# Gathering the experts' tokens by indirect DMA instead of one-hot products, with pairs overlapped by one and a larger weight ring

## The chip, the core and the metric

The kernel runs on one core of one Trainium2 chip. The metric is the device time of one execution in microseconds (us). The core has five engines with an instruction queue each: TensorE (PE, its weight loads PEld), VectorE (DVE), ScalarE (ACT), GpSimd (POOL) and SyncE (SP, which here mainly issues DMAs). ScalarE and POOL can issue DMAs too. Instructions of one queue start in order; between engines, semaphores decide.

## The reference

Two blocks in a row work on 512 tokens of width 1024. The first block (two layers of attention and MLP) and the mixer of the second aren't touched. The change lies in the second block's mixture of experts, which is the last part:

```python
    g_idx = jnp.argmax(g_logits, axis=-1)
...
    top_v, top_i = lax.top_k(e_sel, TOP_K)
    gate = jax.nn.softmax(top_v, axis=-1) * p_g[:, None]
...
    def run(args):
        tok_b, e = args
        xb = v_pad[tok_b]
        hu = xb @ w_e_in[e]
        a, u = jnp.split(hu, 2, axis=-1)
        return (jax.nn.silu(a) * u) @ w_e_out[e]
...
    ys = ys * rows_w[:, None].astype(ys.dtype)
    out = jnp.zeros((T + 1, D), ys.dtype).at[rows_tok].add(ys)
```

A token's group is one of 4, and its two experts are the best of the group's 8. For each of the 32 experts e, w_e_in[e] is 1024 x 1024 and w_e_out[e] 512 x 1024, all in float32. The results, weighted by the gates, are added to the tokens, and a last RMS norm follows.

## The kernel before

The 32 experts are worked in 16 pairs, q = 0 to 15. In a pair each expert has 64 places for tokens; one expert of pair 8 (`SPARE` = 16) is chosen for having most tokens and has a further job of 128 places, the overflow job. More overflow is handled by a loop at the end that runs as often as needed.

`project` comes first. For each of four tiles t of 128 tokens it makes the output product of the mixer (`product`, lines 1410 to 1412) and adds it to `acc` (L1416); `norm` squares (L1421) and makes the root; `flip` transposes `acc` on TensorE (L1434); `logits` multiplies by the router; `select` finds group and experts on VectorE (L1549 to L1590, among them the small TENSOR_SCALAR L1577), `route` numbers the places (L1598 to L1602), and `rows` writes the normalised tokens as two parts, vrh and vrl, for products in two passes: ScalarE makes vrh (L1450), and vrl comes from VectorE for t = 0, 1 (L1452) and from POOL for t = 2, 3 (L1456, after ScalarE's copy L1455). The tiles follow each other without a gap on TensorE: `flip` of one tile stands inside the `product` of the next.

For two pairs at a time, `prepare` makes one-hot tables P of tokens to places on VectorE (`places`), and `gather` multiplies vrh and vrl by them (`collect`, L1735, 64 products of 128 x 256 a time), which gives the transposed tokens X (`store`, L1744 and L1746, times the norm's gain). `expert` then makes the hidden products pa and pu (L1761, 64 a pair, each of two experts on half of the array's columns), the gated activation H, transposes H (L1781), makes the output products py (L1789, 32), scales them by the gate into yh and yl (L1794, L1795), and scatters them into `acc` by the table PT (L1802 to L1804). These steps are generators, and the loop over q in `moe` interleaves them: the scatter of one pair runs beside the hidden products of the next, the gather of pairs q + 2 and q + 3 between the two halves of q and q + 1.

Weights come from `moe_weights`: tiles of 512 KB (128 x 1024 float32), 16 of e_in and 8 of e_out a pair, 384 in all, into a ring of 3 tiles wraw and 26 tiles ew, in the order in which they are used. All are issued by SP (L1523, the last ones as halves, L1527), in order; a load waits until the tile in its place has been used. Part of the ring lies where the mixer's tiles `wo` and `mix` lay, so those loads wait for the last products that read these. Every DMA of the kernel, whichever engine issues it, has one of eight counters, DMAHW0 to DMAHW7, dealt in turn in the order of the program, and waits until the DMA that had this counter before has landed.

## Time and profile before

| what | value |
|---|---|
| median of three runs | 2528.14 us (2528.12 to 2528.62) |
| the profiled execution | 2530.76 us |
| its span in the profile | 2529.0 us |
| mean granted clock of TensorE | 0.989 of full speed |
| TensorE busy | 2458.7 us, 97% of the span |
| VectorE, ScalarE, POOL busy | 59%, 46%, 4% of the span |
| moved by DMA | 361.67 MB, mean 143 GB/s |

A time is counted from the start of the span. `project` starts near 1927, the first expert's hidden products near 2000, and the end of the span is 2529. The profile's two strips of 40 slices (63 us each) show how DMA and TensorE share this last part: TensorE stands at 9 tenths nearly everywhere, and the DMA strip rises from 1 to 3 tenths to 5 to 9 only in the last ten slices, that is from about 1900 on.

The tables by stretches further down have a line for each stretch: its bounds, its length, then for each engine its busy time and, in brackets with an x, its instructions, in the order PE, PEld, DVE, ACT, POOL; then the mean granted clock of TensorE as a share, the DMA engines' busy share and what they moved in GB/s. Where a line of code is chosen, the busy times are those of that line's instructions alone (PE and PEld for a product). A row of a timeline gives the start, the length, engine, line, operation, out<-in by the program's names, shapes and the count; brackets at its end give the idle time before it and who ended it. For SP's queue the length of a row with a count spans all of its issues.

### The profile page before, as it was taken

The page shows a single profiled execution, that of the slowest core. Times are in us where ns is not written, and L with a number is a line of the kernel's source. Part 1 is how long each engine was busy: PE and PEld are TensorE (multiplying, and loading weights), DVE is VectorE, ACT ScalarE, POOL GpSimd, SP SyncE. Part 2 cuts the span into 40 slices and gives each one's busy share as a digit, 9 for nine tenths or more (in the row PEclk, how much of TensorE's full clock was granted, in tenths as well). Part 3 has the DMA queues.
Part 4 walks back from the last instruction along what each step waited for, and adds up shares of the span by engine and source line. Part 5 has one row for each costly group of instructions (what it writes and reads, how often), then busy time and mean ns, then how long its engine had stood idle before and what let it go on. Part 6 is the DMA issues. An engine that isn't in the chain of part 4 may idle for free. (4 is left out here: it accounts for less than half of the span.)

```text
span 2529.0 us, 38832 instructions
## 1 busy us (share of the span) xinstructions
PE 2458.7 (97%) x15048; PEld 1981.4 (78%) x15048; DVE 1480.9 (59%) x2797; ACT 1150.9 (46%) x2181; POOL 98.3 (4%) x83
## 2 busy tenths in 40 slices
PE   8999999999989899999999999999999999999997
PEld 8999999999977777788887988998888744444442
DVE  6666654344589986533445658888653654434435
ACT  6777643233367776422334656655553311112112
POOL 0000000000133220000000000000000000000000
PEclk9999999999999999999999999999999999999998
DMA  3111232222321113232333212121336599978995
GB/s 119 51 51 39 72 93 91 92 92 92 119 69 44 50 35 107 95 100 92 93 99 116 69 59 67 59 67 55 97 120 238 209 394 406 409 297 336 409 409 211
DMA packets 110139, 361.67 MB, mean 143 GB/s; under 512 B 13440, under 2 KB 17792, under 8 KB 109952
## 3 DMA queue, kind: packets, MB, share of 16 engines
q1 hardware_dynamic: 109376, 357.05, 39.7%
q8 instruction: 120, 1.97, 0.3%
q10 hardware_dynamic: 576, 2.10, 0.2%
q14 instruction: 67, 0.55, 0.1%
HBM read 352.75 MB, written 6.36 MB: 142 GB/s over the span
## 5 line engine op out<-in xcount | busy, mean ns | idle before, releaser
L172 PE MATMUL dn<-hg_hi,whi 128*128 128x264 f32 (+1 forms) x2096 | 680.3, 325 | 9.2 <-ACT hg_hi L293 6.7
L173 PE MATMUL dn<-hg_lo,whi 128*128 128x264 f32 (+1 forms) x2096 | 666.1, 318 | 2.1 <-DVE hg_lo L294 2.0
L174 PE MATMUL dn<-hg_hi,wlo 128*128 128x264 f32 (+1 forms) x2096 | 666.3, 318 | 0.0
L144 ACT ACTIVATE whi<-wraw 128x1024 fp32r<-128x1024 f32 (+1 forms) x285 | 284.8, 999 | 606.6 <-PE dn L173 529.6
L172 PEld LDWEIGHTS dn<-hg_hi,whi 128*128 128x128 f32 x2096 | 399.9, 191 | 37.6 <-ACT hg_hi L293 6.7
L173 PEld LDWEIGHTS dn<-hg_lo,whi 128*128 128x128 f32 x2096 | 399.8, 191 | 31.7 <-DVE hg_lo L294 4.3
L174 PEld LDWEIGHTS dn<-hg_hi,wlo 128*128 128x128 f32 x2096 | 399.9, 191 | 24.8
L145 DVE TENSOR_TENSOR wlo<-wraw,whi 128x1024 fp32r<-128x1024 f32 (+1 forms) x285 | 332.3, 1166 | 91.8 <-ACT whi L144 90.4
L172 PE MATMUL dn<-rhi,whi 128*128 128x264 f32 (+1 forms) x768 | 247.0, 322 | 2.2 <-DVE h L202 1.7
L174 PE MATMUL dn<-rhi,wlo 128*128 128x264 f32 (+1 forms) x768 | 246.8, 321 | 0.0
L173 PE MATMUL dn<-rlo,whi 128*128 128x264 f32 (+1 forms) x768 | 246.7, 321 | 0.0
L202 DVE TENSOR_TENSOR h<-h,dn 128x264 f32<-128x264 f32 (+1 forms) x120 | 61.8, 515 | 199.6 <-PE dn L174 199.3
L172 PEld LDWEIGHTS dn<-rhi,whi 128*128 128x128 f32 x768 | 144.4, 188 | 14.8 <-DVE h L202 2.9
L173 PEld LDWEIGHTS dn<-rlo,whi 128*128 128x128 f32 x768 | 144.5, 188 | 11.4
L174 PEld LDWEIGHTS dn<-rhi,wlo 128*128 128x128 f32 x768 | 144.5, 188 | 11.1
L1761 PE MATMUL pa<-ew,X 128*64 128x512 f32 (+1 forms) x470 | 130.7, 595 | 1.9 <-DVE H L1766 1.9
L1761 PE MATMUL pu<-ew,X 128*64 128x512 f32 (+1 forms) x470 | 130.6, 594 | 0.0
L367 DVE SCALAR_TENSOR_TENSOR relu<-dn,rstd 128x264 f32<-128x264 f32 (+1 forms) x93 | 48.2, 519 | 130.3 <-PE dn L174 130.3
L1019 DVE SCALAR_TENSOR_TENSOR H<-pa,PTq 128x512 f32<-128x512 f32 x17 | 11.7, 691 | 187.1 <-ACT PTq L1018 173.6
L1789 PE MATMUL py<-ew,HT 128*64 128x512 f32 (+1 forms) x472 | 112.4, 595 | 0.7 <-ACT HT L1783 0.7
L1804 DVE TENSOR_TENSOR acc<-acc,g 128x512 f32<-128x512 f32 x136 | 86.1, 680 | 35.1 <-PE g L1803 35.1
L1016 ACT ACTIVATE PTq<-pa 128x512 f32<-128x512 f32 x17 | 10.2, 597 | 197.5 <-PE pa L1761 197.5
(545 smaller groups left out, 4373.0 us busy)
## 6 DMA issues: line engine op xcount, KB each, us to landing
ew<-e_in SPq DMA_DIRECT2D x228, 512.0 KB, 10.1
ew<-e_out SPq DMA_DIRECT2D x109, 512.0 KB, 10.1
wraw<-mlp_in SPq DMA_DIRECT2D x64, 512.0 KB, 3.5
wraw<-mlp_out SPq DMA_DIRECT2D x64, 512.0 KB, 3.4
wraw<-w SPq DMA_DIRECT2D x60, 512.0 KB, 3.5
wraw<-e_in SPq DMA_DIRECT2D x28, 512.0 KB, 10.1
wraw<-a_qkv SPq DMA_DIRECT2D x24, 512.0 KB, 3.5
wraw<-kv SPq DMA_DIRECT2D x16, 512.0 KB, 3.5
```

The source lines that it names most:

```text
L144: nc.scalar.activation(hi, raw, AF.Copy)
L145: nc.vector.tensor_sub(lo, raw, hi)
L172: nc.tensor.matmul(ps, whi[:, k, :], hi[:, a:b], start=(k == 0), stop=False)
L173: nc.tensor.matmul(ps, whi[:, k, :], lo[:, a:b], start=False, stop=False)
L174: nc.tensor.matmul(ps, wlo[:, k, :], hi[:, a:b], start=False, stop=(k == len(act) - 1))
L202: self.nc.vector.tensor_add(self.h[:, t, a:b], self.h[:, t, a:b], ps)
L367: nc.vector.scalar_tensor_tensor(x, ps, 0.0, self.rstd[:, a:b], op0=ALU.max, op1=ALU.mult)
L1016: nc.scalar.activation(t, x, AF.Abs)
L1019: nc.vector.scalar_tensor_tensor(out, x, 0.0, t, op0=ALU.min, op1=ALU.subtract)
L1761: nc.tensor.matmul(ps[r], X[i][:, k, :], win[i][k][:, c:c + 512], start=(k == 0), stop=(k == KT - 1), skip_group_check=True)
L1789: nc.tensor.matmul(ys[c][r], HT[:, k, r], wout[i][k][:, c * 512:c * 512 + 512], start=(k == 0), stop=(k == 3), skip_group_check=True)
L1804: nc.vector.tensor_add(self.acc[:, t, cs], self.acc[:, t, cs], po)
```

## The change

`rows` now makes a float32 copy x of every tile of tokens on ScalarE (L1458), multiplies it on POOL by -0.5 times the norm's gain (`grow`, L1463), and writes it to a DRAM buffer `vbuf` by a DMA of ScalarE's queue (L1464). `prepare` now belongs to one job: it makes PT as before, then the token number of each place (`at`) by one more pass over PT with an accumulator, clears a tile `rows` on POOL (L1757) and fills it by an indirect DMA of POOL's queue from `vbuf` (L1758), in which places without a token have an index out of bounds and are skipped. `tokens` transposes `rows` by eight TensorE transposes (L1773) and copies into X. The one-hot products stay only for pairs 0 and 1. The generators are gone: the loop takes jobs 0 to 8, the overflow, 9 to 15, and for job n issues hidden(n), then turned(n-1) (the transposes of H), tokens(n+1), scatter(n-2), prepare(n+2), results(n-1). The loads are reordered accordingly, with a pair's e_in ahead of the e_out of the pair before. The ring has 31 instead of 26 ew tiles, 34 places in all; vrh and vrl move to a pool that ends with `project`.

```diff
-        self.vr = [rp.tile([128, 4, D], F32R, name="vr" + nm) for nm in "hl"]
+        self.vr = [rt.tile([128, 4, D], F32R, name="vr" + nm) for nm in "hl"]
+        gr = rt.tile([128, D], F32, name="grow")
+        src = self.w["g_ffn"]
+        nc.sync.dma_start(gr, bass.AP(tensor=src.tensor, offset=src.offset, ap=[[0, 128], [1, D]]))
+        nc.gpsimd.tensor_scalar(gr, gr, -0.5, None, op0=ALU.mult)
...
         def rows(t):
             hi, lo = self.vr[0][:, t, :], self.vr[1][:, t, :]
             nc.scalar.activation(hi, self.acc[:, t, :], AF.Copy, scale=rs[t])
+            x = rt.tile([128, D], F32, name="vrow", bufs=2)
+            nc.scalar.activation(x, self.acc[:, t, :], AF.Copy, scale=rs[t])
             if t < self.RP:
                 nc.vector.scalar_tensor_tensor(lo, self.acc[:, t, :], rs[t], hi, op0=ALU.mult, op1=ALU.subtract)
             else:
-                x = rt.tile([128, D], F32, name="vrow")
-                nc.scalar.activation(x, self.acc[:, t, :], AF.Copy, scale=rs[t])
                 nc.gpsimd.tensor_sub(lo, x, hi)
+            nc.gpsimd.tensor_mul(x, x, gr)
+            nc.scalar.dma_start(self.vbuf[t * 128:(t + 1) * 128, :], x)
...
-        for q, i in [(q, i) for q in range(14) for i in range(2)] + [(14, 0), (15, 0), (14, 1), (15, 1)]:
-            yield from load(q, *sides[i], 2 if (q, i) == (15, 1) else 1)
+        jobs = self.jobs()
+        for q, p in zip(jobs + [None], [None] + jobs):
+            if q is not None:
+                yield from load(q, self.w["e_in"], KT, 1)
+            if p is not None:
+                yield from load(p, self.w["e_out"], 4, 2 if p == 15 else 1)
...
+    def prepare(self, slot):
...
+        nc.vector.tensor_scalar(q, self.kb[:, 0, :], slot, None, op0=ALU.is_equal)
+        nc.vector.scalar_tensor_tensor(PT, self.kb[:, 1, :], slot, q, op0=ALU.is_equal, op1=ALU.add)
+        nc.vector.scalar_tensor_tensor(q, PT.bitcast(F32), 1.0, self.tok, op0=ALU.mult, op1=ALU.mult,
+                                       accum_out=gs[:, 3:4])
+
+        at = wk.tile([128, 1], U32, name="at", bufs=2)
+        nc.vector.tensor_scalar(at, gs[:, 3:4], float(S), None, op0=ALU.add)
+        rows = wk.tile([128, D], F32, name="rows", bufs=2)
+        nc.gpsimd.memset(rows, 0.0)
+        nc.gpsimd.indirect_dma_start(out=rows, out_offset=None, in_=self.vbuf,
+                                     in_offset=bass.IndirectOffsetOnAxis(ap=at, axis=0), bounds_check=S - 1,
+                                     oob_is_err=False)
...
+    def tokens(self, rows, X, banks):
...
+            for k in range(4):
+                nc.tensor.transpose(ps[:, k * 128:(k + 1) * 128], rows[:, (4 * c + k) * 128:(4 * c + k + 1) * 128],
+                                    self.ident)
...
-    NE, NWO, NXF, NXH = 26, 5, 3, 7
+    NE, NWO, NXF, NXH = 31, 5, 3, 7
...
+            H[n] = self.hidden(win, xs.pop(n), 6 - 2 * (n % 2))
+            if n == 0:
...
+                for i in range(3):
+                    get(i)
+                continue
+            p = jobs[n - 1]
+            HT = self.turned(H.pop(n - 1), 2)
...
+                self.tokens(got[n + 1][2], xs[n + 1], (3, 1))
+            if n > 1:
+                scatter(n - 2, (free, free + 1, 2, 3))
+            get(n + 2)
+            wout = kept[1] if p is None else next(weights)
...
+            y[n - 1] = self.results(HT, wout, got[n - 1][1])
```

Three places of the built order show what moves. The number behind a name is that of the buffer; a bracket lists the semaphores that the instruction waits for, counters of engines or the DMAHW counters. First SP's loads of the first weights, before (loads 18 to 25 of the weights, while the projection ends):

```order
L1523 DMA ew_20182<-e_out 128x1024 [waits DMAHW4_49,PE_49]
L1523 DMA ew_20184<-e_out 128x1024 [waits DMAHW5_49]
L1523 DMA ew_20186<-e_out 128x1024 [waits DMAHW6_49,PE_49,Pool_49]
L1523 DMA ew_20188<-e_out 128x1024 [waits DMAHW7_49]
L1523 DMA ew_20190<-e_out 128x1024 [waits DMAHW0_49]
L1523 DMA ew_20192<-e_out 128x1024 [waits DMAHW1_49]
L1523 DMA ew_20194<-e_out 128x1024 [waits DMAHW2_49,PE_49]
L1523 DMA ew_20247<-e_in 128x1024 [waits DMAHW3_49]
```

and after (the third load into wraw and ring loads 1 to 10):

```order
L1530 DMA wraw<-e_in 128x1024 [waits DMAHW6_49,DVE_49]
L1530 DMA ew_20022<-e_in 128x1024 [waits DMAHW3_49]
L1530 DMA ew_20024<-e_in 128x1024 [waits DMAHW4_49]
L1530 DMA ew_20026<-e_in 128x1024 [waits DMAHW5_49]
L1530 DMA ew_20028<-e_in 128x1024 [waits DMAHW6_49]
L1530 DMA ew_20030<-e_in 128x1024 [waits DMAHW7_49]
L1530 DMA ew_20032<-e_in 128x1024 [waits DMAHW0_49,PE_49]
L1530 DMA ew_20034<-e_in 128x1024 [waits DMAHW1_49]
L1530 DMA ew_20036<-e_in 128x1024 [waits DMAHW2_49,PE_49]
L1530 DMA ew_20038<-e_in 128x1024 [waits DMAHW3_49]
L1530 DMA ew_20040<-e_in 128x1024 [waits DMAHW4_49,PE_49]
```

The four writes of `vbuf` hold DMAHW7, 0, 1 and 2 just ahead of these ring loads in the deal, so that the loads ew_20030 to ew_20036 take over these four counters; all that follows them is issued by SP in order.

Second, ScalarE's last two tiles of the projection, before (vrh, the copy, the square and root of the last tile, and two instructions of the gates, L1608 and L1610):

```order
L1450 ACTIVATE vrh<-acc,vst_19731 128x1024 [waits DVE_49]
L1455 ACTIVATE vrow<-acc,vst_19731 128x1024
L1421 ACTIVATE vrow,vst_19814<-acc 128x1024 [waits DMAHW5_49,DVE_49,Pool_49]
L310 ACTIVATE vst_19814<-vst_19814 128x1 [waits DVE_49]
L311 ACTIVATE vst_19814<-vst_19814 128x1 [waits Activation_49]
L312 ACTIVATE vst_19814<-vst_19814 128x1 [waits Activation_49]
L1450 ACTIVATE vrh<-acc,vst_19814 128x1024 [waits DVE_49]
L1455 ACTIVATE vrow<-acc,vst_19814 128x1024
L1608 ACTIVATE c_19398<-c_19398 128x16 [waits DVE_49]
L1610 ACTIVATE top<-top 128x4 [waits DVE_49]
```

and after (the same steps, with the third and fourth write of `vbuf`; L1622 and L1624 are the former L1608 and L1610):

```order
L1456 ACTIVATE vrh<-acc,vst_19738 128x1024 [waits DVE_49]
L1458 ACTIVATE vrow<-acc,vst_19738 128x1024 [waits DMAHW7_49]
L1430 ACTIVATE vsq,vst_19823<-acc 128x1024 [waits DVE_49]
L1464 DMA vbuf<-vrow 128x1024 [waits DMAHW1_49,Pool_49]
L310 ACTIVATE vst_19823<-vst_19823 128x1 [waits DVE_49]
L311 ACTIVATE vst_19823<-vst_19823 128x1 [waits Activation_49]
L312 ACTIVATE vst_19823<-vst_19823 128x1 [waits Activation_49]
L1456 ACTIVATE vrh<-acc,vst_19823 128x1024 [waits DVE_49]
L1458 ACTIVATE vrow<-acc,vst_19823 128x1024 [waits DMAHW0_49]
L1622 ACTIVATE c_19394<-c_19394 128x16 [waits DVE_49]
L1624 ACTIVATE top<-top 128x4 [waits DVE_49]
L1464 DMA vbuf<-vrow 128x1024 [waits DMAHW2_49,Pool_49]
```

The third write stands behind the last square, the fourth behind both instructions of the gates.

Third, POOL from the start of the projection on, before (index patterns, then the two subtractions, then the next stage):

```order
L1848 IOTA slots 64x16
L1848 IOTA slots 64x16 [waits Pool_49]
L1851 IOTA pcol 128x1 [waits Pool_49]
L1556 IOTA io 128x32
L1456 TENSOR_TENSOR vrl<-vrow,vrh 128x1024 [waits Activation_49] x2
L1679 IOTA Pq 128x16 [waits DVE_49,PE_49]
```

and after (the scaled gain, then multiplications and subtractions of the four tiles, then token numbers and the first gather):

```order
L1393 TENSOR_SCALAR grow<-grow 128x1024 [waits DMAHW1_49,DVE_49,PE_49]
L1463 TENSOR_TENSOR vrow<-vrow,grow 128x1024 [waits Activation_49,Pool_49]
L1463 TENSOR_TENSOR vrow<-vrow,grow 128x1024 [waits Activation_49]
L1462 TENSOR_TENSOR vrl<-vrow,vrh 128x1024 [waits Activation_49]
L1463 TENSOR_TENSOR vrow<-vrow,grow 128x1024 [waits DMAHW7_49,Pool_49]
L1462 TENSOR_TENSOR vrl<-vrow,vrh 128x1024 [waits Activation_49]
L1463 TENSOR_TENSOR vrow<-vrow,grow 128x1024 [waits DMAHW0_49,Pool_49]
L1881 IOTA tok 128x512 [waits DVE_49,PE_49]
L1757 MEMSET rows 128x1024 [waits DVE_49]
L1757 MEMSET rows 128x1024 [waits DMAHW1_49]
L1758 DMA rows<-vbuf,at 128x1024 [waits DMAHW2_49,DVE_49,Pool_49]
```

Four multiplications of 128 x 1024 have come between, and after them the memsets and gathers.

## Rows read from the trace of the kernel before

**Rows 1.** The table by stretches of 20 us, whole engines:

```profile
1960.00:1980.00 20.00, 19.76 (x113) 16.76 (x112) 15.40 (x54) 8.05 (x15) 2.38 (x1) 1.00 0.31 111
1980.00:2000.00 20.00, 16.01 (x94) 15.15 (x96) 13.76 (x66) 6.21 (x13) 2.34 (x1) 0.74 0.43 158
2000.00:2020.00 20.00, 20.00 (x116) 11.31 (x117) 6.56 (x16) 4.70 (x8) 0.00 (x0) 1.00 0.85 325
...
2240.00:2260.00 20.00, 20.00 (x124) 11.45 (x124) 4.40 (x10) 2.46 (x6) 0.00 (x0) 1.00 0.71 281
2260.00:2280.00 20.00, 18.13 (x53) 8.87 (x50) 9.58 (x18) 3.09 (x5) 0.00 (x0) 0.91 0.50 181
2280.00:2300.00 20.00, 20.00 (x97) 11.37 (x96) 12.95 (x27) 5.41 (x9) 0.00 (x0) 1.00 0.60 239
2300.00:2320.00 20.00, 20.00 (x82) 7.21 (x81) 1.96 (x3) 2.53 (x4) 0.00 (x0) 1.00 0.91 351
...
2480.00:2500.00 20.00, 20.00 (x94) 8.40 (x94) 10.01 (x19) 4.95 (x8) 0.00 (x0) 1.00 0.74 267
```

**Rows 2.** The timeline of SP's queue, 1930 to 2002: start, length, line, operation, count:

```profile
1932.99 15.73 SPq L1523 DMA_DIRECT2D ew<-e_in  x13
1949.63 30.48 SPq L1523 DMA_DIRECT2D ew<-e_out  x8
1980.16 2.64 SPq L1523 DMA_DIRECT2D ew<-e_in  x5
2001.84 2.04 SPq L1523 DMA_DIRECT2D wraw<-e_in  x3
```

**Rows 3.** The page's part on DMA issues: count, KB each, us to landing:

```profile
ew<-e_in SPq DMA_DIRECT2D x228, 512.0 KB, 10.1
...
out<-acc SPq DMA_DIRECT2D x4, 512.0 KB, 3.3
```

**Rows 4.** The timeline of ScalarE: first scaling of results, two pairs, four apart:

```profile
2120.81 0.69 ACT L1794 ACTIVATE yh<-py,gs 128x512 fp32r<-128x512 f32 x1 [7.95 <-PE py L1789]
...
2239.61 0.69 ACT L1794 ACTIVATE yh<-py,gs 128x512 fp32r<-128x512 f32 x1 [7.93 <-PE py L1789]
```

**Rows 5.** Those four pairs as one stretch, lines 1761, 1789, 1735 alone, in turn:

```profile
2120.81:2239.61 118.80, 55.61 (x256) 18.39 (x256) 1.00 1.03 409
...
2120.81:2239.61 118.80, 28.35 (x130) 8.84 (x128) 1.00 1.03 409
...
2120.81:2239.61 118.80, 16.38 (x128) 15.57 (x128) 1.00 1.03 409
```

**Rows 6.** The timeline of POOL in the projection; in brackets idle before, releaser:

```profile
1977.41 2.38 POOL L1456 TENSOR_TENSOR vrl<-vrow,vrh 128x1024 fp32r<-128x1024 f32 x1 [49.35 <-ACT vrow L1455]
1987.78 2.34 POOL L1456 TENSOR_TENSOR vrl<-vrow,vrh 128x1024 fp32r<-128x1024 f32 x1 [7.99 <-ACT vrow L1455]
```

**Rows 7.** The timeline of VectorE in the projection:

```profile
1970.31 0.23 DVE L1577 TENSOR_SCALAR og<-io,idg 128x4 f32<-128x4 f32 x1
...
1977.42 2.39 DVE L1577 TENSOR_SCALAR og<-io,idg 128x4 f32<-128x4 f32 x1
...
1981.94 0.68 DVE L1416 TENSOR_TENSOR acc<-acc,g 128x512 f32<-128x512 f32 x1
...
1989.49 0.65 DVE L1550 SCALAR_TENSOR_TENSOR c<-R,gm,io 128x4 f32<-128x4 f32 x1
```

**Rows 8.** The timeline of ScalarE there: two instructions, last tile:

```profile
1982.70 1.06 ACT L1421 ACTIVATE vrow<-acc 128x1024 f32<-128x1024 f32 x1 [5.38 <-issue]
...
1993.79 0.20 ACT L1610 ACTIVATE top<-top 128x4 f32<-128x4 f32 x1 [2.36 <-DVE top L1609]
```

**Rows 9.** The timeline of TensorE: end of the projection, and the last pair:

```profile
1982.68 0.93 PE L1434 MATMUL g<-ident,acc 128*128 128x128 f32 x4 [2.92 <-DVE acc L1416]
...
2487.56 7.04 PE L1789 MATMUL py<-ew,HT 128*64 128x512 f32 x32
...
2507.43 1.08 PE L1789 MATMUL py<-ew,HT 128*64 128x512 f32 x4
```

More of the change, by code (lines that the diff above doesn't have):

```diff
@@ L1806, in expert @@
-        if last:
+        if scatter:
             for k in range(4):
@@ L1928, in moe, with scatter @@
+        def scatter(n, banks):
+            for c in range(2):
+                self.scatter(got[n][0], y[n][c], c, banks)
+        kept = None
+        for n, q in enumerate(jobs):
+            if n == self.QSWAP:
                 self.swap()
-            if q == self.QSWAP + 1:
+            if n == self.QSWAP + 1:
                 self.spread(self.key, self.kb)
                 self.tables()
-            if q % 2 == 0 and 2 * q != self.SPARE:
-                work = prepare(q + 2) if q < 14 else none
-                next(work, None)
@@ L1998, in moe @@
         with tc.For_i(0, more, 1):
-            for Xw, sl in overflow(self.base[:, 0:1]):
-                pass
-            for _ in self.expert(self.block_weights(), [Xw[:, :, :128]], sl):
-                pass
+            PT, gate, rows = self.prepare(further(self.base[:, 0:1]))
+            ws, X = self.block_weights(), xtile()[:, :, :128]
+            self.tokens(rows, X, (3, 1))
+            HT = self.turned(self.hidden(next(ws), X, 4), 2)
+            y = self.results(HT, next(ws), gate)
+            for c in range(2):
+                self.scatter(PT, y[c], c, (6, 7, 2, 3))
             shift()
```

276 lines of the change are left out of this document (105 added, 171 removed).

## The prediction

> **What bounds the kernel now.** I read first the table by stretches [rows 1]. TensorE is busy for 20 of 20 us in most stretches, with two holes: 1980 to 2000 (16.01 us, at a mean granted clock of 0.74, so in part at the lower of its two levels) and 2260 to 2280 (18.13). The DMA queues run at 409 GB/s through most of the experts and sag twice: 111 and 158 GB/s between 1960 and 2000, and 281, 181, 239 and 351 between 2240 and 2320. The first sag costs nothing, since by then the ring is full: SP issued 26 loads between 1933 and 1983 [rows 2], after three more into wraw, which makes the 29 places, and issued the next only at 2001.84, when the first expert freed some. The second sag is the overflow job: it uses no new weights, so the ring stays full; (409-281)/409 of 20 us and so on make 6.3 + 11.1 + 8.3 + 2.8 = 28.5 us of unused DMA time.
>
> So two limits lie close together. A pair of experts takes TensorE (2239.61 - 2120.81)/4 = 29.7 us [rows 4]; its 24 loads of 512 KB take the queues 24 x 0.524 MB / 409 GB/s = 30.8 us, 1.28 us a load (the 409 GB/s: [rows 5]). TensorE sets the pace only because 29 loads (37 us) are there before the first expert starts, near 2000. It never waits long for a weight up to the last product at 2507.43 [rows 9], and from there to the end of the span, 2529.0, there are 21.6 us that the change leaves alone. Whoever lightens TensorE finds the queues 1 us behind it; what counts is when the queues may start and what more they carry.
>
> **The change part by part.**
>
> TensorE loses the gather products: line 1735 holds it for 16.38 us in four pairs, 4.1 a pair [rows 5]. It gains eight transposes a pair; four took 0.93 us at the low clock [rows 9], so at most 1.9. A pair then takes 27 us, below the 30.8 of its loads. VectorE loses the place tables and gains one pass and one copy a pair; it was busy 2 to 13 of 20 us there [rows 1], so this is nothing on the path.
>
> The queues gain the gathers. Only chosen rows move: 512 tokens twice, 1024 x 4 KB = 4.2 MB or 10.3 us at 409 GB/s. No row shows an indirect transfer. Lower bound 0 (they fall into DMA time that is idle anyway), upper bound all 17 tiles whole, 8.9 MB or 22 us; I take 10.3, since unused places are skipped. Their waiting costs nothing: from the release of a tile of rows to its use lies a whole pair, 27 us or more, against 3.3 to 10.1 us from issue to landing for the same size [rows 3]. The first gather of use, the third, can't start before routing is done and may stop TensorE for such a landing time once, but then the queues are what is late, and 34 places let them run 34 x 1.28 = 43.6 us on.
>
> The start of the loads moves, and this decides. In the new order each transfer takes the next of eight counters and waits until the transfer that had it before has landed. The four new writes of vbuf, on ScalarE's queue, stand in that order between the third and the fourth load. The eighth load of all (ew_20030) thus waits for the first of these writes, the tenth for the third, the eleventh (ew_20036) for the fourth, and SP issues in order. Ten loads are out until the fourth write has landed, instead of 29. Before, loads went on through the whole projection [rows 2].
>
> When does that write land? In ScalarE's new order it stands behind the instruction that ran at 1993.79, to 1993.99 [rows 8]. It also waits for POOL: the subtraction, as before (1987.78 to 1990.12 [rows 6]), and a new multiplication of the same shape, 2.36 us. And the chain ahead grows. The subtraction of 1977.41 lasted 2.38 us, and VectorE's small TENSOR_SCALAR of 1977.42 lasted 2.39 us, where its like of 1970.31 took 0.23 [rows 6, 7]: a hold of 2.16 us. Behind it came late the addition of 1981.94, and behind that the 2.92 us in which TensorE had nothing [rows 7, 9] and after which the clock was low. At the second subtraction the hold was shorter (0.65 us for a small instruction). The change has four multiplications, one per tile, each beside this same chain, whose additions TensorE's transposes and ScalarE's squares wait for. Four holds of 0.4 to 2.16 us make 1.7 to 8.6; I take 8.6, since three of the four meet the very instruction that was held for 2.16. Then 1993.99 + 8.6 + 3.3 for landing [rows 3] gives 2006. Without any hold it would be 1990.12 + 2.36 + 3.3 = 1996.
>
> The Trainium skill, on its page "SBUF — State Buffer", section "Who interferes with whom", says that GpSimd and VectorE share a port pair that is locked for a whole instruction, and whichever comes second is blocked fully; VectorE needs it for tensor_scalar and for two inputs in SBUF. The 2.39 us agree. By that rule each multiplication holds up to its whole 2.36 us, 9.4 in all, and the landing would be at 2007; without the rule it is 1996, which is a rival below.
>
> The sum, for the queues as the limit: 384 loads less 10 make 374 x 1.282 = 479.4 us from 2006, to 2485.4. Gathers 10.3: 2495.7. Then what is left of the overflow's sag. The four kept output loads of the ninth pair are given back when the overflow's output products use them. From the start of these loads to that, TensorE has 2 us for a landing, 0.9 to end a product, two times hidden products at 55.61/4 = 13.9 [rows 5], one time output products at 28.35/4 = 7.1, two times scatter and transposes (29.7 - 13.9 - 7.1 - 4.1 = 4.6, and 2 to 3 for transposes and VectorE's additions in a row, so 7.4), and 1.8 for the first release: 54. The ring runs 34 loads on, 43.6 us. Some 10 to 11 us are left; 11, with 0 to 14 as bounds (0 if TensorE is ahead there, 14 if it is 3 late): 2506.7. Landing of the last load, 2 us: 2508.7. Tail: the last input load comes 16 loads (20.5 us) ahead of the last one. Before, from the end of the hidden products to the last product it was 2507.43 - 2487.56 = 19.9 us [rows 9]; the new order puts one more scatter and transposes between, 6 us, and 0.9 to end the hidden products: 26.8, so 6.3 behind the last landing. The last product stands at 2515.0, the span ends 21.6 later: 2536.6, which is 7.6 above 2529.0. The profiled run's own time, 2530.76, is 1.8 above its span and 2.6 above the median of 2528.14; 2528.1 + 7.6 gives **2536**.
>
> **The rivals.**
>
> Faster, by an earlier start: the holds don't add up (the landing is at 1996, 10 earlier), the sag is gone (11 less), and half the gather bytes fall into idle DMA time (5 less). That gives 2536 - 26 = 2510; with one or the other alone, 2520 to 2526. For it speaks that TensorE has 4 us a pair in hand to be early at the overflow, and the hold of only 0.65 us. Against it: if the queues are the limit, TensorE can't be early there.
>
> Faster, because the writes don't stop the loads (the change then brings nearly what its larger ring could: TensorE at 27 us a pair). The ring is full at the first expert, the queues have 350 loads left from about 2006: 448.7 + 10.3 + 11 + 2 + 6.3 + 21.6 gives a span of 2506. Against it is the order of the built program; only an early landing of the writes can undo it.
>
> No change: landing at 1998 to 2000 with the other terms as they are, 2529 to 2531. The point from which it decides is the hold per multiplication: at 0.4 to 0.7 us it is so.
>
> Slower still: unused places move too, or each gather's rows slow the loads as much as whole tiles would. Then 22 instead of 10.3 us, and 2548; with a second drop of the clock at the end of the projection, 2552.
>
> **How the numbers follow.** The forecast, 2531 to 2541, gets 0.50; the earlier start 0.17 (half of it under 2520); loads not stopped 0.05; no change 0.15; slower still 0.13. From no change a measurement here can tell about 0.2%, 5 us: faster is below 2523, slower above 2533.2. The forecast lies above this for all but 0.06, so slower has 0.44 + 0.13 = 0.57, the same 0.15 + 0.06 = 0.21, faster 0.22. For 8 in 10 the range reaches down to 2516, which leaves out 0.12, and up to 2550.
>
> **What would show it.** In the profile after: ten loads by about 1990 and the eleventh at 2003 to 2009, where rows 2 have 26; DMA at 0 to 160 GB/s from 1940 to 2000 and 409 without a dip from about 2010 to 2300; one sag of some 11 us near 2300 to 2330, not four stretches; TensorE idle before loads in most pairs, with the waits ended by DMA, not by VectorE; POOL's multiplications with a small VectorE instruction of about 2.4 us beside each; rows' transposes waiting only in the first gathered pair. The prediction is wrong if SP's eleventh load goes out before 1998, if the hidden products of the first pair start no later than 2000, or if TensorE and not the queues is busy throughout the pairs.

## The result, and the profile after

The kernel after takes 2544.49 us (median of four runs, 2543.79 to 2548.4); the kernel before, on the same chip, 2528.38 (2528.12 to 2528.78). The ratio is 1.0067, with a 95% interval of 1.0049 to 1.0084: 16 us slower. The forecast was 2536, with a range of 2516 to 2550. So the direction and the range held, and the size was missed by half: 16.1 us instead of 7.6.

The profiled execution took 2543.79 us, its span 2541.7. From the page of the kernel after: busy time and share of each engine, the DMA strip in GB/s (slices of 63.5 us), and the DMA queue of the gathers with packets and MB:

```profile
PE 2438.9 (96%) x14656; PEld 1931.7 (76%) x14656; DVE 1479.5 (58%) x2759; ACT 1141.2 (45%) x2166; POOL 153.0 (6%) x122
...
GB/s 120 54 53 30 80 92 92 92 91 88 134 59 50 43 34 118 92 99 92 94 97 116 67 59 59 65 61 59 104 125 139 255 408 409 408 402 303 408 409 241
...
q0 software_dynamic: 2448, 4.20, 0.4%
```

TensorE lost 20 us of busy time, and the kernel still grew. From the 33rd slice on the strip stands at 402 to 409, but for one slice of 303 and the last. The gathers moved 4.20 MB.

The table by stretches of the kernel after (columns as in [rows 1]):

```profile
1940.00:1960.00 20.00, 19.11 (x99) 15.83 (x97) 7.21 (x16) 5.03 (x9) 3.43 (x1) 1.00 0.00 0
1960.00:1980.00 20.00, 15.90 (x94) 13.41 (x94) 16.21 (x49) 9.10 (x16) 6.67 (x3) 1.00 0.30 106
1980.00:2000.00 20.00, 16.51 (x90) 15.91 (x91) 14.16 (x55) 4.37 (x9) 5.87 (x3) 0.66 0.26 85
2000.00:2020.00 20.00, 19.25 (x106) 9.10 (x106) 5.76 (x13) 6.29 (x12) 2.35 (x3) 1.00 1.00 400
...
2260.00:2280.00 20.00, 19.08 (x65) 7.83 (x64) 11.19 (x23) 1.76 (x3) 1.67 (x2) 1.00 1.00 388
...
2300.00:2320.00 20.00, 19.07 (x91) 8.37 (x88) 6.47 (x12) 3.50 (x7) 0.95 (x1) 1.00 0.39 154
2320.00:2340.00 20.00, 20.00 (x79) 7.23 (x79) 6.64 (x15) 1.37 (x2) 1.46 (x1) 1.00 0.86 326
...
2500.00:2520.00 20.00, 20.00 (x89) 8.72 (x88) 10.67 (x19) 3.10 (x5) 0.00 (x0) 1.00 0.62 218
...
2513.00:2514.00 1.00, 1.00 (x6) 0.29 (x4) 0.54 (x1) 0.00 (x0) 0.00 (x0) 1.00 0.56 225
```

Read the last number of each line. While the projection ends (1940 to 2000), the DMA engines now move 0, 106 and 85 GB/s. Then they run at 400 to 411 up to 2300, but for the 388 from 2260 to 2280 with which the sag at the overflow begins. There is one sag where [rows 1] have four stretches: (409-388) + (409-154) + (409-326), over 409 and times 20, makes 17.6 us. From 2500 to 2520 the engines move 218 x 20 us = 4.4 MB. That would be 10.7 us at 408 GB/s, but the rate is lower there, and the last data comes in the last line, about 0.55 us after 2513: data ends near 2513.6.

Why so little moves before 2000 is seen in SP's queue. Its timeline in the kernel after (start, length, line, operation, count), which answers [rows 2], and below it its waits from 1930 to 2010 (us in total, times, longest):

```profile
1929.81 5.82 SPq L1530 DMA_DIRECT2D ew<-e_in  x4
...
1961.84 0.33 SPq L1530 DMA_DIRECT2D ew<-e_in  x1
...
1985.47 0.33 SPq L1530 DMA_DIRECT2D ew<-e_in  x1
...
1998.51 1.75 SPq L1530 DMA_DIRECT2D ew<-e_in  x4
```

```profile
SPq L1530 <- DMA vbuf<-vrow: 60.5, 4, 26.2
```

After three loads into wraw and four into ew, the eighth, ninth, tenth and eleventh load each wait for one of the four writes of `vbuf`: four waits, 60.5 us. The eleventh goes out at 1998.51. The write that it waits for is issued by ScalarE behind the second gate instruction, as [rows 8] let expect. ScalarE's timeline in the kernel after:

```profile
1995.69 0.21 ACT L1624 ACTIVATE top<-top 128x4 f32<-128x4 f32 x1 [2.36 <-DVE top L1623]
1995.75 0.33 ACTq L1464 DMA_DIRECT2D vbuf<-vrow  x1
```

That the queues, and not TensorE, then set the pace agrees with the pair's length. ScalarE's timeline, first scaling of results, two pairs, four apart (compare [rows 4]):

```profile
2111.08 0.69 ACT L1822 ACTIVATE yh<-b,gs 128x512 fp32r<-128x512 f32 x1 [10.44 <-PE b L1817]
...
2238.90 0.69 ACT L1822 ACTIVATE yh<-b,gs 128x512 fp32r<-128x512 f32 x1 [10.43 <-PE b L1817]
```

A pair takes (2238.90 - 2111.08)/4 = 31.96 us instead of 29.7, at 408 GB/s throughout: 24 loads and a gather. That TensorE could be faster is shown further down, where the same work takes 27.0 to 27.6 us a pair.

**Where the 16 us come from.** The start of the projection, SP's load of `wr`, stood at 1926.84 in the profile of before and at 1922.09 in that of after, though the code ahead of it is the same. Over the profiled executions here it lies anywhere from 1921.2 to 1927.3. The granted clock of TensorE goes with it: from 40 to 60 and from 710 to 910 its mean is 0.91 and 0.94 in the profile of before, 1.00 and 0.96 in that of after, which is some 6 us of full clock. So from here on I count from that load to the end of the span ("from start to end"): 602.2 us before, 619.6 after, 17.4 more. That is near the 16.1 of the medians, and it leaves out the shift ahead of the projection. It rests on one profiled execution of each kernel, though, and the clock differs behind the start too, so I give the medians beside it. The forecast by the same count, term by term:

| term, us | forecast | after |
|---|---|---|
| projection start to SP's eleventh load | 79.2 | 76.4 |
| from there to the end of the data | 502.7 | 515.1 |
| end of the data to the last product | 6.3 | 6.5 |
| last product to the end of the span | 21.6 | 21.6 |
| sum | 609.8 | 619.6 |

The experiments ask three things: whether the queues set the end, what exactly holds the loads, and what the kernel is worth when nothing does.

### The profile page after: what moved, and what is told of

Read it like the earlier page. It is cut to its first block, busy times and chain, and to the rows that moved or that the text cites. A ratio compares the mean times of both kernels' runs of the same rounds, so it can differ in the third digit from the quotient of the medians.

```text
span 2541.7 us, 38126 instructions
## 1 busy us (share of the span) xinstructions
PE 2438.9 (96%) x14656; PEld 1931.7 (76%) x14656; DVE 1479.5 (58%) x2759; ACT 1141.2 (45%) x2166; POOL 153.0 (6%) x122
## 3 DMA queue, kind: packets, MB, share of 16 engines
q0 software_dynamic: 2448, 4.20, 0.4%
## 5 line engine op out<-in xcount | busy, mean ns | idle before, releaser
L1790 PE MATMUL b<-ew,X 128*64 128x512 f32 (+1 forms) x964 | 251.3, 598 | 6.6 <-DMA ew<-e_in 6.5
L1790 PEld LDWEIGHTS b<-ew,X 128*64 128x64 f32 (+1 forms) x964 | 79.2, 138 | 168.3 <-issue 116.0
L1019 DVE SCALAR_TENSOR_TENSOR H<-b,lsg 128x512 f32<-128x512 f32 x17 | 11.7, 691 | 236.9 <-ACT lsg L1018 236.9
L1016 ACT ACTIVATE lsg<-b 128x512 f32<-128x512 f32 x17 | 10.2, 597 | 246.7 <-PE b L1790 246.7
L1817 PE MATMUL b<-ew,HT 128*64 128x512 f32 (+1 forms) x476 | 116.0, 603 | 1.7 <-DVE X L1777 1.7
L1822 ACT ACTIVATE yh<-b,gs 128x512 fp32r<-128x512 f32 x34 | 23.4, 687 | 171.5 <-PE b L1817 171.0
## 6 DMA issues: line engine op xcount, KB each, us to landing
wraw<-e_in SPq DMA_DIRECT2D x23, 512.0 KB, 10.5
```

Source lines behind the costliest of these rows:

```text
L1016: nc.scalar.activation(t, x, AF.Abs)
L1019: nc.vector.scalar_tensor_tensor(out, x, 0.0, t, op0=ALU.min, op1=ALU.subtract)
L1790: nc.tensor.matmul(ps[r], X[:, k, r], w[k][:, c:c + 512], start=(k == 0), stop=(k == KT - 1), skip_group_check=True)
L1817: nc.tensor.matmul(ys[c][r], HT[:, k, r], w[k][:, c * 512:c * 512 + 512], start=(k == 0), stop=(k == 3), skip_group_check=True)
L1822: nc.scalar.activation(yh, ys[c], AF.Copy, scale=gate)
```

## Do the queues set the end?

**More bytes, same work** (e11_all_rows). Empty places get a row too.

```diff
-        nc.vector.tensor_scalar(at, gs[:, 3:4], float(S), None, op0=ALU.add)
+        nc.vector.tensor_scalar(at, gs[:, 3:4], float(S), float(S - 1), op0=ALU.add, op1=ALU.min)
```

> The changed kernel, but a place without a token fetches row 511 of vbuf instead of being skipped (its gate is zero), so that every gather moves all of its 128 rows: 17 x 512 KB = 8.9 MB instead of the 4.2 MB that the software queue of the profile shows, 4.7 MB or 11.5 us more at 409 GB/s. Theory Q (the queues set the end of the changed kernel): 10 to 14 us slower, 2554 to 2558. Rival P (TensorE sets it, gathers are hidden): within 3 of 2544. Rival (the gathers' cost is their issue and landing, not their bytes): within 3 of 2544 too, with TensorE's waits for rows unchanged.

Measured: 2555.33 us, ratio 1.0102 [1.0087, 1.0118], that is 10.8 above after's median (7.5 from start to end). The page of this run:

```profile
q0 software_dynamic: 2448, 8.91, 0.9%
```

The same number of packets carry 8.91 MB instead of 4.20. The 4.71 MB more are 11.5 us at 408 GB/s, and two thirds (7.5) to nine tenths (10.8) of that reach the end. This also settles that unused places are skipped in the kernel after: only chosen rows move.

**More TensorE work, same bytes** (e12_pe_more). Each transpose of rows is made three times.

```diff
-                nc.tensor.transpose(ps[:, k * 128:(k + 1) * 128], rows[:, (4 * c + k) * 128:(4 * c + k + 1) * 128],
-                                    self.ident)
+                for _ in range(3):
+                    nc.tensor.transpose(ps[:, k * 128:(k + 1) * 128],
+                                        rows[:, (4 * c + k) * 128:(4 * c + k + 1) * 128], self.ident)
```

> The changed kernel, but every transpose of the gathered rows is made three times into the same place: 16 more transposes of about 0.11 us a job, 1.7 to 2 us a pair, some 26 us of TensorE time in all. Theory Q: TensorE waits for loads, so most of it is hidden: 0 to 6 us slower, 2544 to 2550 (the stretch around the overflow, where TensorE is late, is what shows). Rival P: 22 to 28 us slower, 2566 to 2572.

Measured: 2548.95, ratio 1.0077 [1.0062, 1.0093], 4.5 above after's median (2.7 from start to end) for some 26 us of TensorE time. The stretch from 2120 to 2240, once of after and once of this kernel:

```profile
2120.00:2240.00 120.00, 112.98 (x467) 42.53 (x468) 47.96 (x95) 18.47 (x32) 8.86 (x8) 1.00 1.03 408
```

```profile
2120.00:2240.00 120.00, 116.58 (x530) 49.87 (x528) 45.40 (x85) 17.99 (x30) 7.74 (x7) 1.00 1.03 408
```

The rate is 408 in both; TensorE is busier, 116.58 against 112.98, and the time is nearly the same. Bytes count, TensorE's time hardly does. That part of the forecast stands.

**A smaller ring** (e5_ring26).

```diff
-    NE, NWO, NXF, NXH = 31, 5, 3, 7
+    NE, NWO, NXF, NXH = 26, 5, 3, 7
```

> The changed kernel with 26 instead of 31 ring tiles. By the built order the writes of vbuf then hold the loads later in the row: sixteen loads are out before the fourth write lands instead of ten. Theory Q: six loads more at the start give 7 to 8 us, five places fewer make the DMA sag at the overflow 5 x 1.28 = 6.4 us longer (16.5 before, then 22 to 24): together 2541 to 2545, the two cancelling, both to be read from the DMA columns. Rival (the ring's size doesn't matter because loads are always late): sag unchanged and 2536 to 2538. Rival P: no change in time and no relation between sag and time.

Measured: 2545.89, ratio 1.0071 [1.0054, 1.0088], 0.9 us shorter from start to end (1.4 longer by the medians). The table of this kernel at the overflow:

```profile
2260.00:2280.00 20.00, 20.00 (x65) 8.31 (x62) 5.37 (x13) 2.39 (x4) 1.46 (x1) 1.00 0.72 270
...
2300.00:2320.00 20.00, 19.08 (x78) 8.88 (x73) 10.76 (x22) 3.35 (x6) 2.41 (x2) 1.00 0.21 72
2320.00:2340.00 20.00, 19.61 (x86) 7.78 (x85) 3.21 (x5) 4.72 (x8) 0.95 (x1) 1.00 1.01 393
```

The sag is 24 us instead of 17.6, since five places are five loads of 1.28 us less to run on with. It costs nothing in sum, because in this ring 16 loads instead of ten were out before the fourth write. The five places added by the change bring 6.5 us at the overflow; the order that came with them takes that back at the start.

## What holds the loads?

**The writes on POOL's queue** (e1_pool_queue). In the built order these writes wait for POOL alone and use none of the eight counters of SP's loads: DMAs that POOL issues have counters of their own, and only those of SP and ScalarE share the eight.

```diff
-            nc.scalar.dma_start(self.vbuf[t * 128:(t + 1) * 128, :], x)
+            nc.gpsimd.dma_start(self.vbuf[t * 128:(t + 1) * 128, :], x)
```

> The changed kernel, but POOL's queue writes vbuf instead of ScalarE's, so that the ring loads no longer follow those writes on a DMAHW counter. Theory Q (the queues set the end and the loads start too late, held by the shared counters): the eleventh load goes out near 1977 instead of 1999, held now only by products that read the place's old content and by POOL's last subtraction near 1991; 17 to 20 loads are out at 1999 instead of 10, so the time falls by 8 to 13 us to 2532 to 2537. Rival P (TensorE's own work in the new order sets the end, the loads are late but not what is waited for): 2544, within 3. Rival M (the counters hold nothing that the places' old content wouldn't hold as long): eleventh load within 3 us of 1999, 2544.

Measured: 2543.68, ratio 1.0061 [1.0044, 1.0078], only 3.8 us shorter from start to end (0.8 by the medians). The expected gain of 8 to 13 didn't come. SP's timeline and its waits from 1930 to 2010 in this kernel tell why:

```profile
1975.88 5.81 SPq L1530 DMA_DIRECT2D ew<-e_in  x6
...
2002.65 6.63 SPq L1530 DMA_DIRECT2D ew<-e_in  x11
```

```profile
SPq L1530 <- PE b L1421: 42.4, 3, 39.2
SPq L1530 <- DVE p L1723: 18.8, 1, 18.8
...
SPq L1530 <- PE b L1730: 2.1, 1, 2.1
```

Loads don't wait for writes any more. They wait up to 1975.88 for the last of the mixer's products (L1421), whose operands lay in their places, and fourteen are out by 1981.7. But the fifteenth goes out only at 2002.65. It waits 18.8 us for VectorE's one-hot tables of the first two pairs (L1723) and 2.1 more for the products that read the parts vrh and vrl (L1730). Its place covers the index pattern `kio`, from which the tables are made, and the start of vrh: both lie in the pool that ends with `project`. The built order of the kernel after shows it, in a row further down than the ones that I showed before the prediction:

```
L1530 DMA ew_20044<-e_in 128x1024 [waits DVE_49,DMAHW6_49,PE_49,Pool_49]
```

So there is a second hold behind the first, and it ends at the same time. It is part of the change too: vrh, vrl and `kio` have moved to that pool, and the ring grew over it. Fourteen loads instead of ten are ahead, 4 x 1.28 = 5.1 us, and the next goes out 77.6 us after the projection's start instead of 76.4: 3.9 us, near the 3.8 measured.

**The ring laid out otherwise** (e2_ring_order). The places on that pool now come last in the ring; the writes stay on ScalarE's queue.

```diff
-        return self.ew.tile([128, D], F32, name="ew%d" % ((i + self.NFREE) % self.NE))
+        order = list(range(18, 23)) + list(range(18)) + list(range(23, self.NE))
+        return self.ew.tile([128, D], F32, name="ew%d" % order[i])
```

> The changed kernel, but the first ring loads go to the places in another order (18 to 22, 0 to 17, 23 to 30 instead of 18 to 30, 0 to 17), whose old content is read for the last time some 25 us earlier; counters stay shared with the vbuf writes. Theory Q, counters: the eleventh load still waits for the fourth write, near 1999, and the time stays at 2544, within 3. Rival M (old content of the places holds the loads): the eleventh load goes out before 1980 and the time falls by 10 us or more.

Measured: 2549.77, ratio 1.0084 [1.0067, 1.0101]; from start to end 0.6 longer than after. (The median stands 5 us higher; in its profile the projection starts 5.0 later, at 1927.10.) SP's eleventh load and its waits in this kernel:

```profile
2003.41 6.62 SPq L1531 DMA_DIRECT2D ew<-e_in  x11
```

```profile
SPq L1531 <- DMA vbuf<-vrow: 61.3, 4, 25.8
```

The eleventh load leaves 76.3 us after the start, as in after. Lifting the second hold alone gives nothing.

**Both** (e3_both): the two edits together.

```diff
-        return self.ew.tile([128, D], F32, name="ew%d" % ((i + self.NFREE) % self.NE))
+        order = list(range(18, 23)) + list(range(18)) + list(range(23, self.NE))
+        return self.ew.tile([128, D], F32, name="ew%d" % order[i])
...
-            nc.scalar.dma_start(self.vbuf[t * 128:(t + 1) * 128, :], x)
+            nc.gpsimd.dma_start(self.vbuf[t * 128:(t + 1) * 128, :], x)
```

> The changed kernel with both edits at once: vbuf written from POOL's queue, and the ring places taken in the order 18 to 22, 0 to 17, 23 to 30. Theory Q+M (each of the two holds, the shared counters and the places' old content, hides the other: the places 29 and 30 lie on vrl, read by the last gather products until about 2001): 20 loads are out by 1965 and more than 30 before the first hidden product, the time falls by 7 to 13 us to 2531 to 2537, not by the whole 25 us of lead, since TensorE's stop before the third pair's tokens and its 29 us a pair then come to bear. Rival P (TensorE alone sets the end): 2544 within 3. Rival Q alone: 2519 to 2524.

Measured: 2524.42 over ten runs, ratio 0.9981 [0.9971, 0.9991]; from start to end 595.8 us, 23.9 shorter than after (20.1 by the medians; the profile is of the fastest of the ten runs). This is faster than the 2531 to 2537 that I had expected of the pair, and close to the rival that only the queues count (2519 to 2524). SP's timeline and the table while the projection ends:

```profile
1928.87 57.05 SPq L1531 DMA_DIRECT2D ew<-e_in  x29
```

```profile
1940.00:1960.00 20.00, 18.52 (x97) 15.39 (x97) 8.09 (x18) 5.40 (x10) 4.21 (x2) 1.00 0.64 237
1960.00:1980.00 20.00, 15.56 (x93) 13.06 (x91) 16.26 (x48) 8.74 (x16) 8.23 (x4) 1.00 0.45 156
1980.00:2000.00 20.00, 17.33 (x94) 16.59 (x96) 13.52 (x56) 5.13 (x12) 6.77 (x6) 0.66 0.86 339
2000.00:2020.00 20.00, 19.88 (x108) 9.11 (x106) 6.29 (x19) 5.52 (x11) 1.58 (x3) 1.00 1.00 382
```

32 loads, three of them into wraw, are out by 1986. From 1940 to 2020 the lines add up to 1114 x 20 us against 591 x 20 in after: 10.5 MB, or 25.6 us at 408 GB/s, and the end comes 23.9 earlier. One hold alone was worth 3.8, the other -0.6, both together 23.9 (by the medians 0.8, -5.3 and 20.1). This is what two equal holds in a row look like: each hides the other, and an experiment that lifts one seems to refute it.

## What do the multiplications cost?

**No multiplication on POOL** (e4_no_mul): the rows are written as they are, and the gain is applied when X is copied, in eight copies instead of two.

```diff
-            nc.gpsimd.tensor_mul(x, x, gr)
...
-            if c:
-                nc.vector.tensor_copy(y, p3)
-            else:
-                nc.scalar.activation(y, p3, AF.Copy)
+            for k in range(4):
+                g = self.gains[:, 6 * KT + 4 * c + k:6 * KT + 4 * c + k + 1]
+                if c:
+                    nc.vector.tensor_scalar(y[:, k, :], p3[:, k, :], g, None, op0=ALU.mult)
+                else:
+                    nc.scalar.activation(y[:, k, :], p3[:, k, :], AF.Copy, scale=g)
```

> The changed kernel without POOL's multiplications and without the gain's tile: vbuf holds the plain normalised rows, and the gain goes in where tokens copies the transposed rows, eight copies of 128x128 instead of two of 128x512. Theory Q with the hold on VectorE: the four holds of about 2 us go (the part from the start of the projection to the first hidden product is 7 us shorter), the fourth write no longer waits for POOL, so the eleventh load goes out at 1984 to 1990 instead of 1999; the sag at the overflow grows by a few us since the first product is less late; 2530 to 2538. Rival (POOL's work is hidden beside the projection): the projection as long as in the changed kernel and 2541 to 2546.

Measured: 2540.85, ratio 1.0046 [1.0029, 1.0063], 7.0 shorter than after from start to end (3.6 by the medians), where I had expected 2530 to 2538; the first hidden product comes 72.9 us after the projection's start instead of 79.0 (before: 73.1). So the multiplications cost the projection 6.0 us. Where they do, VectorE's and POOL's timelines in the kernel after show:

```profile
1955.64 1.28 DVE L1460 SCALAR_TENSOR_TENSOR vrl<-acc,vst,vrh 128x1024 fp32r<-128x1024 f32 x1
1957.03 2.17 DVE L1591 TENSOR_SCALAR og<-io,idg 128x4 f32<-128x4 f32 x1
...
1966.84 2.36 DVE L1591 TENSOR_SCALAR og<-io,idg 128x4 f32<-128x4 f32 x1
```

```profile
1955.75 3.43 POOL L1463 TENSOR_TENSOR vrow<-vrow,grow 128x1024 f32<-128x1024 f32 x1 [26.81 <-ACT vrow L1458]
...
1990.54 2.38 POOL L1463 TENSOR_TENSOR vrow<-vrow,grow 128x1024 f32<-128x1024 f32 x1
```

Beside each of the four multiplications stands a small VectorE instruction of 2.05 to 2.36 us, where its like without POOL beside it takes 0.23 [rows 7]. Both end together: 1955.75 + 3.43 and 1957.03 + 2.17 are 1959.18 and 1959.20. In the kernel without multiplications the same line takes its short time (VectorE's timeline):

```profile
1962.44 0.23 DVE L1586 TENSOR_SCALAR og<-io,idg 128x4 f32<-128x4 f32 x1
```

The end moves by more than the projection: this kernel's eleventh load goes out 67.0 us after the start, 9.4 earlier than in after. Its sag at the overflow is 2 us longer, which leaves some 7.

## What is left when nothing holds the loads?

**All three edits** (e6_all): e1, e2 and e4 together.

> The changed kernel with three edits: vbuf written from POOL's queue, ring places in the order 18 to 22, 0 to 17, 23 to 30, and no multiplication on POOL (the gain goes in where tokens copies the transposed rows, in eight copies of 128x128). Theory Q+M with TensorE close behind: the projection is 7 us shorter and 30 loads are out before the first hidden product, so TensorE now sets the pace, at about 29 us a pair, with one stop of 8 to 13 us before the first gathered tokens: 2530 to 2535, slightly slower than the kernel before; DMA sags again in two places, as before the change. Rival Q alone: 2512 to 2520.

Measured: 2527.19 over ten runs, ratio 0.9993 [0.9983, 1.0003], 602.9 from start to end. So taking the multiplication out of e3's kernel makes the projection 5.8 us shorter and gains nothing: by the medians this kernel is 2.8 us slower, and the intervals of the two ratios overlap. The two profiles are 7.1 us apart from start to end, and nearly all of that goes with the granted clock. From 2010 to 2330, once of e3_both and once of this kernel:

```profile
2010.00:2330.00 320.00, 302.62 (x1374) 125.14 (x1372) 148.43 (x331) 58.14 (x98) 31.80 (x28) 0.99 0.97 384
```

```profile
2010.00:2330.00 320.00, 298.03 (x1324) 122.26 (x1320) 143.59 (x342) 62.42 (x129) 30.31 (x27) 0.97 0.94 368
```

A mean of 0.97 instead of 0.99 over 320 us is some 6 us of full clock. So the two profiles don't show what the eight copies cost. With the loads out early the end is no longer set by the queues alone: the sags at the overflow are 28 us together (e3: 19), and a pair takes 28.2 us instead of 27.6. The eight copies do stand in the chain now. One of TensorE's waits between 2010 and 2490 in this kernel:

```profile
PE b L1848 <- ACT X L1777: 6.0, 14, 0.6
```

Its scatter products wait 14 times for X's copy, 6.0 us in all; in e3_both they never do.

**Two gathers less, the third first** (e7_all_skip): pairs 0 and 1 take their tokens from the one-hot products, so their gathers are left out, and pair 2 is prepared ahead of them. The rest as in e6_all; `prepare` now fetches rows only where its last argument is true.

```diff
-                got[n] = self.prepare(further(1024.0 * self.SPARE + self.CAP) if q is None else slots[:, q:q + 1])
+                got[n] = self.prepare(further(1024.0 * self.SPARE + self.CAP) if q is None else slots[:, q:q + 1],
+                                      n > 1)
...
-                for i in range(3):
+                for i in (2, 0, 1):
                     get(i)
```

> The three edits (writes of vbuf from POOL's queue, ring order, no multiplication on POOL), and pairs 0 and 1 prepare only their scatter table and gate, no gather, with the third pair prepared first. If TensorE now sets the pace, its stop before the first gathered tokens shrinks from about 11 to 3 us and the time falls by 5 to 8 us against the kernel with the three edits alone: 2524 to 2530. If the queues still set it, the two gathers are only 0.5 MB, 1.3 us: 2530 to 2534.

Measured: 2518.52 over seven runs, ratio 0.9963 [0.9952, 0.9975]; 8.7 below e6_all's median (12.8 from start to end), more than expected. The table shows what else went. From 2040 to 2060, first e6_all, then this kernel:

```profile
2040.00:2060.00 20.00, 17.25 (x70) 6.42 (x70) 7.68 (x22) 4.28 (x9) 0.95 (x1) 0.73 0.93 348
```

```profile
2040.00:2060.00 20.00, 20.00 (x100) 7.63 (x98) 1.99 (x3) 2.57 (x4) 0.00 (x0) 0.98 1.03 409
```

In e6_all TensorE stands for 6.8 us before the first gathered rows, and after that its mean granted clock is 0.73 for 20 us, which means partly the lower of its two levels (1.2 and 2.4 GHz), and the queues move 348 GB/s. With the third pair prepared first there is no such wait, the clock is 0.98, and the rate 409. The kernel after has the wait too, 6.8 us, and a clock of 0.76 from 2040 to 2060, but its queues stay at 408 GB/s: there it costs nothing, because the queues are what is late.

**The scatter in two halves** (e8_inter): as e7_all_skip, and the second half of the scatter of pair n-2 is put between the two scalings of the results of pair n-1, so that the products of the two halves no longer follow each other.

```diff
-                scatter(n - 2, (free, free + 1, 2, 3))
+                self.scatter(got[n - 2][0], y[n - 2][0], 0, (free, free + 1, 2, 3))
...
-        for c in range(2):
-            weigh(c)
+        weigh(0)
+        rest()
+        weigh(1)
         return y
```

> As the kernel with four edits (vbuf from POOL's queue, ring order, no multiplication on POOL, no gather for pairs 0 and 1), and the scatter of a pair in two halves, one ahead of the output products and one behind them, so that each half has four banks of its own and TensorE waits no more for VectorE's additions. If TensorE sets the pace: 29 us a pair fall to 27, the queues take over at about 31, and the time falls by another 12 to 20 us to 2506 to 2516, below the kernel before. If the queues set it already: no more than 3 us.

Measured: **2508.76**, ratio 0.992 [0.9902, 0.9938]: 20.8 us faster than the kernel before on that chip (2529.53), and the best version here. The pair takes 27.0 us. TensorE's waits for VectorE's additions between 2010 and 2490, 13.5 us in e7_all_skip, are 0.6 here. TensorE's time is worth something again once the queues may start early.

**The same with the multiplication** (e10_mul): e8's edits, but the gain applied by POOL as in the change.

> Four edits to the changed kernel: vbuf written from POOL's queue, ring places in the order 18 to 22, 0 to 17, 23 to 30, no gather for pairs 0 and 1, and the scatter in two halves around the output products. POOL's multiplication by the gain stays, so the projection is 6 us longer than in the kernel that has these edits without the multiplication (2508.8), but tokens makes two copies instead of eight. If the queues set the end there, the loads' start counts, which the projection's length moves by 6 us only where the places are held by its last reads: 2508 to 2514. If TensorE's copies count (the kernel with the three edits and eight copies was no faster than the one with the two and the multiplication): 2498 to 2506.

Measured: 2513.61, ratio 0.9941 [0.9928, 0.9955]. From start to end it is 4.5 longer than e8_inter (4.9 by the medians), with a projection 6.8 longer. So the change's idea wins 16 us with its multiplication and 21 without.

## Why the prediction was right, and where it was off

**What bounds.** Right. After the change the queues set the end; e11 and e12 show it, and the pair went from 29.7 to 31.96 us while TensorE's own work in it shrank. One sign that I named was wrong: I wanted to see TensorE idle before loads, with the waits ended by DMA and not by VectorE. Its three largest waits between 2010 and 2490 in the kernel after:

```profile
PE b L1850 <- DVE acc L1851: 12.9, 28, 0.5
PE b L1773 <- DMA rows<-vbuf,at: 6.8, 1, 6.8
PE b L1790 <- DMA ew<-e_in: 6.1, 29, 0.2
```

29 waits for weights, none longer than 0.2 us, 6.1 in sum; twice as much for VectorE's additions behind the scatter; and TensorE is busy 19 of 20 us in the table. By its busy share one would take it for the bound, by its waits VectorE. The DMA column and the experiments say otherwise: with 26 us more work in e12_pe_more the waits for VectorE fall to 3.7 us and the time hardly moves.

**The eleventh load.** The step said that ten loads are out until the fourth write lands and that the eleventh leaves 79.2 us after the projection's start. It left after 76.4. (The sign was named as 2003 to 2009 of the span's time, and the profile has 1998.51; with the start of before it would be 2003.3.) The holds were forecast at 4 x 2.16 = 8.6 and measured (from the durations above 0.23 of the four VectorE instructions beside the multiplications) at 1.9 + 2.1 + 1.9 + 1.8 = 7.8. Not all of that reached the fourth write: it was issued 73.7 us after the start, 6.5 later than the end of the gate instruction in before (67.2), and landed within 2.8 us instead of 3.3. The rule named with it, from the page "SBUF — State Buffer", section "Who interferes with whom", of the Trainium skill, holds in both directions here: POOL's first multiplication lasted 3.43 instead of 2.38 us beside VectorE's 1.28 us instruction with two inputs.

**Only the counters hold the loads.** This was half of the truth. The step took it that, without the waits for the writes, the loads would run on as in [rows 2]; the rival "the writes don't stop the loads" was priced at 2506 on that ground. In e1_pool_queue the writes don't stop the loads, and the time is 2543.68: the places on the pool that ends with the projection hold them as long. I had read the semaphores of the first loads only, not of the fifteenth. The forecast time did not suffer, since both holds end together, and that was luck: nothing in the prediction made sure of it. The rival's price did suffer.

**The gathers.** 4.2 MB were forecast and 4.20 moved. The rows' wait came once, 6.8 us, in the first gathered pair, as said.

**The overflow's sag.** This is the term that was mis-sized most: 11 us forecast, 17.6 measured, beyond the bound of 14. TensorE's timeline in the kernel after through the overflow, SP's longest wait from 2295 to 2330, and what the queue of the loads moved from 2262 to 2312 (packets, MB):

```profile
2264.51 3.65 PE L1817 MATMUL b<-ew,HT 128*64 128x512 f32 x16
...
2271.53 14.00 PE L1790 MATMUL b<-ew,X 128*128 128x512 f32 x32
...
2319.87 7.03 PE L1817 MATMUL b<-ew,HT 128*128 128x512 f32 x16
```

```profile
SPq L1530 <- PE b L1817: 21.8, 3, 20.6
```

```profile
q1 hardware_dynamic: 4926, 17.91, 90.6%
```

The four kept tiles come free 1.8 us into the products of 2319.87, as forecast, and data flows again at about 2323.3. (The 2 us of the forecast for a load to begin had no row behind them; here they are 1.5, from the issue at 2321.78.) The 34 loads that the ring allows, 17.83 MB, end with the data that stops near 2307.5 and, by the bytes, begin at 2262.2: that is where the first kept tile's data came. From there to 2323.3 are 61.1 us; I had 54. The steps in between have the durations that I gave them; what was missing is the start. I let the overflow's hidden products follow at once (2 + 0.9 us), as if TensorE were waiting for just these loads. In truth it is behind them: it had transposes and scatter to do, during which loads run ahead, and only at 2264.51 began the output products of the pair before, which ended at 2271.5, 9.3 us after the kept tile's data began and not 2.9. A stage that is paced by loads in one part of its round is late against them in another.

**The tail.** Forecast 6.3 us from the last data to the last product, measured 6.5, and by the way that was forecast. TensorE's timeline in the kernel after: its last wait for a load, and the last of three rows in [rows 9]:

```profile
2492.73 1.93 PE L1790 MATMUL b<-ew,X 128*64 128x512 f32 x6 [0.21 <-DMA ew<-e_in]
...
2520.08 1.08 PE L1817 MATMUL b<-ew,HT 128*64 128x512 f32 x4
```

From 2492.73 TensorE works for 27.4 us up to its last product without waiting for another load; the forecast had 26.8. From there to the end 21.6 us, as said.

**What stays open.** From the eleventh load to the end of the data it took 12.4 us longer than forecast. The sag makes 6.6 of it, the lower rate behind 2500 2.9 (13.6 us for what would be 10.7), the load of the final gain behind the last weights (0.5 MB) 1.3, and the rate of 408 instead of 409 GB/s 1.2; under 1 us is left. Why the rate falls behind 2500, where only half loads of 256 KB are left, is not shown. Nor is what the eight copies of e6_all cost.

## What to carry to other kernels

Before a transfer is added to a queue, read in the built order which completion counters and which reused places the loads behind it share with it, and read on past the first wait: two holds of equal length hide each other, and lifting either alone shows next to nothing. Where transfers set the end, what counts is the time at which they may start, the bytes they move, and every stretch in which the ring is full; time saved on the engine pays only when the loads can use it. And the busy share of an engine that waits a little before each of many loads doesn't show that it waits: read the length of a round and the transfer rate instead. And before the difference of two single profiles is put down to an edit, compare their granted clocks, and the medians of several runs.

## What the runs showed of the hardware that I had not expected

- POOL is held beside VectorE too, not only VectorE beside POOL: its first multiplication took 3.43 us instead of 2.38.
- A gather in which half of the places are skipped has as many packets as one that moves every row (2448 in both), but half the bytes (4.20 against 8.91 MB); the other half cost 7.5 to 10.8 us, where the bytes alone make 11.5.
- The start of the projection, behind 1920 us of the same code, varied from 1921.2 to 1927.3 us between profiled executions, and the granted clock went with it (from 710 to 910 a mean of 0.94 before, 0.96 after). That is a third of the effect studied here; counting from an event behind the unchanged part removed it.
